# Offering the small instruction streams a place behind every dense product instead of behind every third

## The chip, the cores and the metric

The kernel runs on one core of one Trainium2 chip. The metric is the device time of one execution in microseconds (us), lower is better. The kernel before takes 2010.35 us (median of three runs, 2009.24 to 2010.55).

## What is computed

One layer of an encoder trunk in float32: 1024 tokens of width 1024, with 16 learned tokens in front.

```python
h = rmsnorm(h_res, norm1_w[l])
proj = h @ w_in[l]
(q, k, v, z, b_raw, a_raw, sc_b, sc_c, sc_x, gate_a, gate_b) = jnp.split(proj, SPLIT_POINTS, axis=-1)
o_dn = gated_deltanet_bidir(q, k, v, z, b_raw, a_raw, dn_conv_w[l], A_log[l], dt_bias[l], dn_norm_w[l])
y_a = o_dn @ w_branch_dn[l]
y_b = (sc_b * depthwise_conv_centred(sc_c * sc_x, sc_conv_w[l])) @ w_branch_sc[l]
merged = jax.nn.sigmoid(gate_a) * y_a + jax.nn.sigmoid(gate_b) * y_b
h_res = h_res + merged @ w_out[l]
h2 = rmsnorm(h_res, norm2_w[l])
gu = h2 @ w_gate_up[l]
h_res = h_res + (jax.nn.silu(gu[..., :D_FF]) * gu[..., D_FF:]) @ w_down[l]
```

The gated DeltaNet branch has 8 heads of 128 columns. For each head, q, k and v go through a five-tap convolution and SiLU; the sequence is cut into chunks; in each chunk a triangular system is solved, and a state matrix is carried from chunk to chunk, once forward and once backward:

```python
def step(S, inp):
    qk_c, qd_c, kd_c, u_c, w_c, gl_c = inp
    v_new = u_c - jnp.einsum("bhcd,bhde->bhce", w_c, S)
    o_c = (jnp.einsum("bhcd,bhde->bhce", qd_c, S)
           + jnp.einsum("bhij,bhje->bhie", qk_c, v_new))
    S = S * gl_c[..., None, None] + jnp.einsum("bhcd,bhce->bhde", kd_c, v_new)
    return S, o_c
```

## The kernel before

The change lies in the first stage, from the start to about 1061 us, which holds the input projection and the whole DeltaNet branch. The later stages (the branch projections, the output projection, the MLP) are not touched.

**Dense products.** The input projection is cut into units of 128 output columns. Each unit is computed in two or three runs over the tokens, 320 to 512 tokens wide (336, 320 and 384 for q, k and v; 322, 320 and 384 for two of the three short-convolution columns; 512 for the rest). One run is 24 matmuls into one PSUM bank: 8 pieces of the contraction, and for each the three products of high and low parts that stand for one float32 product. These matmuls are line L339, in `dense_steps`, which is a generator: it yields after every third matmul. ScalarE or VectorE then empties the bank.

**Streams.** Per head there are four generators that issue small work: `g_decay`, `g_norm` (transposes and Gram products of q and k), `g_inv` (the triangular inverse) and `g_scan` (the chunk recurrence, 8 steps per head, both directions in each step). Each yields the planned time at which its next piece may be issued. Of these the scan matters most here. In each step it issues, in this order: TensorE L805 and L808 (state times k and q), VectorE L815 (r), TensorE L820 (inverse times r), ScalarE L827 (w, two instructions) and L832 (v, two instructions), TensorE L837 (k times w, the state's increment) and L840 (the second part of the output), VectorE L849 (the new state) and then output work. L805, L820 and L837 write different columns of the same PSUM bank, `b1`; w and v are both read from the columns that L820 wrote. One float32 matmul of 128 columns runs as two passes, so a pair of them stands as four instructions in the trace.

**The order.** The order on every engine is the order in which the instructions are issued by the Python code; an engine executes its own in that order, and semaphores hold it where an operand is not ready. The code keeps four planned clocks `T`. `pe(ns)` advances that of TensorE and returns the time plus HOP = 200 ns; `V` and `A` advance VectorE's and ScalarE's by a cost for the width and return the end plus TOPE = 370 ns. A scan's wait between L820 and L837 reads so:

```python
            for d in range(2):
                mm(b1[:, 2 + d], NP[:, cd[d], d], r0[d], start=True, stop=True)
            yield pe(430)
```

and then w (whose last `A` gives the time that is yielded), v (whose time is not yielded), and the next yield. At every yield of a dense unit the main loop calls `run_streams`, which issues every stream's piece whose time has come by TensorE's planned clock, and `pump`, which fills VectorE with convolution and inverse work until it is planned 700 ns ahead. So a piece of a stream can stand only where a dense unit yields. The main loop also cuts the next unit's weights into high and low parts at four fixed yields of a unit, numbered in `SPL`: ScalarE L945 (wh), then VectorE L942 (wl), twice.

Of the kernel before, what the change touches and what calls it, by code (L numbers as in the profile page):

```python
# [47 lines left out]
def encoder_layer(ctx: ExitStack, tc: tile.TileContext, x, meta, norm1_w, w_in, w_ba,  # L48
# [22 lines left out]
    def psm():  # L71
        return ps.tile([P, 512], F32, tag="m", name=uid("pm"), bufs=2)
# [37 lines left out]
    def wtiles(shape):  # L110
        return [wp.tile(shape, F32R, tag=g, name=uid(g), bufs=2) for g in ("wh", "wl")]
# [158 lines left out]
    def pe(ns):  # L270
        T["pe"] += ns
        return T["pe"] + HOP

    def V(n, kind=0):
        return on("dve", (68 + 1.042 * n, 130 + 1.042 * n, 130 + 0.52 * n)[kind])

    def A(n):
        return on("act", 144 + 0.834 * n)
# [37 lines left out]
    def pump():  # L316
        while T["dve"] <= T["pe"] + 700:
            now = max(T["dve"], T["pe"])
            cand = [k for k, q in lanes.items() if q and q[0].ready <= now + 20]
            if not cand and any(q and q[0].ready <= now + DEP + 20 for q in lanes.values()):  # L320
                T["dve"] = now + DEP
                continue
            if not cand:
                return
            k = min(cand, key=lambda q: spent[q])
            spent[k] += lanes[k][0].step() * WEIGHT[k]
            if lanes[k][0].done:
                lanes[k].pop(0)

    sweep = ()  # L330

    def dense_steps(po, w, xx, t0, n):
        (wh, wl), (xh, xl) = w, xx
        t0 += C0
        parts = {"hh": (wh, lambda k: xh[:, k]), "hl": (wh, lambda k: xl[k]), "lh": (wl, lambda k: xh[:, k])}
        seq = [(m, k) for m in sweep for k in range(KT)] if sweep else [(m, k) for k in range(KT) for m in ("hh", "hl", "lh")]
        for i, (m, k) in enumerate(seq):
            ww, f = parts[m]
            mm(po[:, :n], ww[:, k], f(k)[:, t0:t0 + n], start=i == 0, stop=i == 3 * KT - 1)  # L339
            if i % 3 == 2:  # L340
                pe(3 * (n / 2.4 + 13))
                yield

    raws = []
# [6 lines left out]
    def half_buffer():  # L351
        return d1.tile([P, 520], F32, tag="rb", name=uid("rb"), bufs=3)
# [20 lines left out]
    def u_qkv(h, i, w):  # L373
# [9 lines left out]
        for ci, (t0, n) in enumerate(QCH):  # L383
            po = psm()
            yield from dense_steps(po, w, hx, t0, n)
            if raw is None:
                raw = row_buffer()
                nc.gpsimd.memset(raw[:, 0:2], 0.0)
                nc.gpsimd.memset(raw[:, L + 2:L + 4], 0.0)
            nc.scalar.copy(raw[:, 2 + t0:2 + t0 + n], po[:, :n])  # L390
            nc.scalar.activation(dst[:, t0:t0 + n], po[:, :n], AF.Copy, scale=wc[:, 2, col:col + 1])  # L391
            A(n)
            A(n)
            yield
            sub["rows"] = 2 + t0 + n if ci < 2 else L + 4
            if ci == 1:
                job = enqueue("conv", conv_job(raw, dst, col, sub, "t"))
                raws.append(job)
# [21 lines left out]
    def u_short(j, i, w):  # L420
        st_ = shorts[j]
        if i < 2:
            for t0, n in ((14, 322), (336, 320), (656, 384)):
                po = psm()
                yield from dense_steps(po, w, hx, t0, n)
                if "cx" not in st_:
                    st_["cx"] = row_buffer()
                    nc.gpsimd.memset(st_["cx"][:, 1026:1028], 0.0)
                    raws.append(Job(iter(())))
                sl = st_["cx"][:, t0 - 14:t0 - 14 + n]  # L430
                if i == 0:
                    nc.scalar.copy(sl, po[:, :n])
                    A(n)
                else:
                    nc.vector.tensor_tensor(out=sl, in0=po[:, :n], in1=sl, op=ALU.mult)
                    V(n)
            if i == 1:
                st_["yc"] = []
                st_["job"] = enqueue("conv", short_job(st_["cx"], j, st_["yc"]))
                raws[st_["ri"]] = st_["job"]  # L440
            else:
                st_["ri"] = len(raws) - 1
        else:
            for i2 in range(2):
                po = psm()
                yield from dense_steps(po, w, hx, META + 512 * i2, 512)
                force(st_["job"])
                yc = st_["yc"][i2][:, :512]
                nc.vector.tensor_tensor(out=yc, in0=po, in1=yc, op=ALU.mult)
                V(512)  # L450
                nc.sync.dma_start(p_d[j][:, 512 * i2:512 * i2 + 512], yc)
# [10 lines left out]
    def u_z(h, w):  # L462

        rest = None
        for i in range(2):
            po = psm()
            for k, _ in enumerate(dense_steps(po, w, hx, META + 512 * i, 512)):
                if k == 3 and rest:
                    rest()
                yield  # L470
            th = half_buffer()[:, :512]
            nc.scalar.activation(th, po, AF.Tanh, scale=0.5)
            A(512)

            def rest(i=i, th=th, po=po):
                nc.vector.scalar_tensor_tensor(out=th, in0=th, scalar=1.0, in1=po, op0=ALU.add, op1=ALU.mult)
                V(512)
                nc.sync.dma_start(z_d[h][:, 512 * i:512 * i + 512], th)
        T["dve"] = max(T["dve"], T["act"] + HOP)
        rest()  # L480
# [275 lines left out]
    def g_scan(h, st_):  # L756
# [141 lines left out]
        for c4 in range(2):  # L898
            oT = NP[:, 4 * c4:4 * c4 + 4, 1 - c4]
            pt = newbank()  # L900
            for c in range(4):
# [10 lines left out]
                 for h in range(H) for i, off in enumerate((OK, OQ, OV))]  # L912
    fill_units = [(off + j * P, lambda w, j=j, i=i: u_short(j, i, w), None, i)
                  for j in range(8) for i, off in enumerate((OSC, OSX, OSB))]
    fill_units += [(off + j * P, lambda w, j=j, d_=d_[j]: u_gate(j, d_, w), None, None)
                   for j in range(8) for off, d_ in ((OGA, ta_d), (OGB, tb_d))]
    fill_units += [(OZ + h * P, lambda w, h=h: u_z(h, w), None, None) for h in range(ZH)]
    done = freed = 0
    decs, norms, invs, scans = [], [], [], []
# [5 lines left out]
    def pick():  # L925

        mid = fill_units and fill_units[0][3] in (1, 2)
        if qkv_units and not mid and qkv_ok():
            u = qkv_units.pop(0)
        elif fill_units:  # L930
            u = fill_units.pop(0)
        else:
            return None
        raw = rawtile([P, KT, P])
        nc.sync.dma_start(raw, w_in[unit(u[0])])
        return [u, None, raw, [0]]

    def split_part(u, i):
        u[3][0] = i + 1
        k = slice(4 * (i // 2), 4 * (i // 2) + 4)  # L940
        if i % 2:
            nc.vector.tensor_tensor(out=u[1][1][:, k], in0=u[2][:, k], in1=u[1][0][:, k].bitcast(F32), op=ALU.subtract)  # L942
            V(512)
        else:
            nc.scalar.copy(u[1][0][:, k], u[2][:, k])  # L945
            A(512)
# [20 lines left out]
    def run_streams():  # L967
        nonlocal done
        again = True
        while again:  # L970
            again = False
            for q in (scans, invs, norms, decs):
                if q and q[0][1] <= T["pe"]:
                    again = True
                    r = next(q[0][0], None)
                    if r is None:
                        h = q.pop(0)[2]
                        if q is scans:
                            done += 1
                        elif q is not decs:  # L980
                            heads[h]["inverted" if q is invs else "normed"] = True
                    else:
                        q[0][1] = r
            start_streams()
# [335 lines left out]
                yield T["act"]  # L1320

    dn = ph1.enter_context(tc.tile_pool(name="dn", bufs=1))
    SPL = (11, 12, 13, 14)
    for g in (gen0, gen1):
        for _ in g:
            pass
    decs.append([g_gates(), T["pe"], None])
    while done < H or qkv_units or fill_units or any(ahead):
        u = ahead.pop(0)
        if u is None:  # L1330
            run_streams()
            pump()
            T["pe"] += 100
            ahead.append(pick())
            continue
        for k in range(u[3][0], 4):
            split_part(u, k)
        if ahead[0]:
            ahead[0][1] = wtiles([P, KT, P])
        ahead.append(pick())  # L1340
        for n_, _ in enumerate(u[0][1](u[1])):
            if ahead[0] and n_ in SPL:
                split_part(ahead[0], SPL.index(n_))
            run_streams()
            pump()
# [240 lines left out]
    for j in range(NF):  # L1586
# [9 lines left out]
        if j >= HK:  # L1596
            k = j - HK
# [176 lines left out]
```

## Time and profile before

| | |
|---|---|
| median of three runs | 2010.35 us |
| the profiled execution's own time | 2009.61 us |
| its span, first to last instruction | 2007.9 us |
| TensorE clock granted, mean | 0.999 |
| TensorE matmul busy | 1987.4 us, 99% of the span |
| VectorE busy | 1353.8 us, 67% |
| ScalarE busy | 823.9 us, 41% |
| dense products of the first stage (L339) | 4272 matmuls |

All times are from one profiled execution; a start time counts from its first instruction. In rows of the timeline the first two numbers are the start and the duration in us, then the engine (PE is TensorE's matmuls, PEld its weight loads, DVE VectorE, ACT ScalarE), the line, the instruction, what it writes and reads, the shape, the count of instructions merged into the row, and in brackets the engine's idle time before it and what ended that. A matmul's duration is longer than its distance to the next, because matmuls are pipelined; what counts is the distance between starts.

### The profile page before, as it was taken

Reading aid. Unit: us, or ns where it says so; the run is one execution under the profiler, and the core shown is the slowest. Engines: PE = TensorE matmul, PEld = TensorE weight load, DVE = VectorE, ACT = ScalarE, POOL = GpSimd, SP = SyncE. Lnnn points to the kernel's source line nnn. Section 1 sums busy time; section 2 is a strip of 40 time slices with the busy share of each in tenths; the row PEclk is TensorE's granted clock in tenths of the full one; section 3 lists DMA queues with packets and bytes.
Section 4 is the critical chain, followed back from the end, with each engine's and each line's share of the span. In section 5 each row is a group of like instructions: output and inputs, shape, how many; then the busy total and the mean of one; then the engine's idle time right before and its main releaser. Section 6 shows DMA issues by size and latency. Waiting matters only on the chain.

```text
span 2007.9 us, 31943 instructions
## 1 busy us (share of the span) xinstructions
PE 1987.4 (99%) x12059; PEld 1727.9 (86%) x12059; DVE 1353.8 (67%) x2966; ACT 823.9 (41%) x1945; POOL 119.6 (6%) x407
## 2 busy tenths in 40 slices
PE   9999999999999999999999999999999999999998
PEld 8999999999999988988888888887888888888887
DVE  6889586888888776866245434468866666646575
ACT  6462345454554464633334211224423333334344
POOL 2002200101020202010000000000000000000000
PEclk9999999999999999999999999999999999999999
DMA  3121222212212232232127633123666345477654
GB/s 138 40 88 64 75 78 71 74 47 76 59 54 85 69 101 64 81 89 94 70 94 247 215 126 116 58 90 109 237 225 221 139 149 186 158 272 244 196 172 167
DMA packets 131409, 247.85 MB, mean 123 GB/s; under 512 B 45045, under 2 KB 54694, under 8 KB 128823
## 3 DMA queue, kind: packets, MB, share of 16 engines
q1 hardware_dynamic: 130679, 244.77, 36.1%
q8 instruction: 94, 1.54, 0.3%
q10 hardware_dynamic: 576, 1.05, 0.1%
q14 instruction: 60, 0.49, 0.1%
HBM read 179.10 MB, written 66.67 MB: 122 GB/s over the span
## 4 chain that ended last, share of the span: by engine, by line
PE 90%; DVE 5%; ACT 2%; DMA 1%; issue 1%; SPq 0%; ACTq 0%; DVEq 0%
PE pm L339 36%; PE pd L1514 10%; PE pe L1514 4%; PE pm L1514 3%; PE pe L589 1%; PE pd L820 1%; PE pe L134 1%; PE pe L135 1%; PE pe L133 1%; PE pd L840 1%; PE pd L134 1%; PE pd L133 1%; PE pd L135 1%; PE pe L1682 1%; PE pe L1680 1%; PE pd L837 1%
## 5 line engine op out<-in xcount | busy, mean ns | idle before, releaser
L339 PE MATMUL pm<-hTh,wh 128*128 128x512 f32 (+4 forms) x1424 | 518.2, 369 | 0.8 <-ACT kq L391 0.5
L339 PE MATMUL pm<-hTh,wl 128*128 128x512 f32 (+4 forms) x1424 | 483.4, 344 | 0.0
L339 PE MATMUL pm<-al,wh 128*128 128x512 f32 (+4 forms) x1424 | 482.6, 343 | 0.0
L339 PEld LDWEIGHTS pm<-hTh,wh 128*128 128x128 f32 x1424 | 267.0, 188 | 20.4 <-issue 1.7
L339 PEld LDWEIGHTS pm<-hTh,wl 128*128 128x128 f32 x1424 | 266.1, 188 | 19.8 <-DVE wl L942 0.3
L339 PEld LDWEIGHTS pm<-al,wh 128*128 128x128 f32 x1424 | 267.4, 189 | 14.5
L101 DVE TENSOR_TENSOR al<-raw,ring_h 128x1024 fp32r<-128x1024 f32 x73 | 88.8, 1224 | 65.4 <-ACT ring_h L100 64.6
L942 DVE TENSOR_TENSOR wl<-raw,wh 128x512 fp32r<-128x512 f32 x134 | 91.0, 690 | 51.0 <-ACT wh L945 50.5
L100 ACT CAST ring_h<-raw 128x1024 fp32r<-128x1024 f32 x73 | 76.8, 1055 | 106.8 <-PE pd L1682 35.5
L361 DVE SCALAR_TENSOR_TENSOR kq<-ra,wc,kq 128x520 f32<-128x520 f32 x128 | 96.9, 757 | 3.3 <-ACT kq L391 1.7
L945 ACT CAST wh<-raw 128x512 fp32r<-128x512 f32 x134 | 79.2, 622 | 13.3 <-PE pm L339 9.6
L100 ACT CAST wh<-raw 128x1024 fp32r<-128x1024 f32 x43 | 45.2, 1052 | 85.8 <-PE pe L134 35.2
L827 ACT ACTIVATE w<-pd,small 128x128 f32<-128x128 f32 x128 | 40.2, 366 | 84.8 <-PE pd L820 79.7
L498 DVE TENSOR_TENSOR fP<-fP,tm 128x135 f32<-128x135 f32 (+23 forms) x248 | 71.3, 288 | 4.9
L494 DVE TENSOR_TENSOR tm<-fP,fN 128x135 f32<-128x135 f32 (+23 forms) x248 | 71.2, 287 | 4.4
L849 DVE SCALAR_TENSOR_TENSOR S<-S,eGl,pd 128x128 f32<-128x128 f32 x104 | 31.9, 345 | 52.0 <-PE pd L837 33.9
L1516 DVE TENSOR_TENSOR b<-pd,b 128x512 f32<-128x512 f32 x22 | 15.2, 691 | 68.5 <-PE pd L1514 68.5
L1617 ACT ACTIVATE b<-b 128x512 f32<-128x512 f32 x22 | 13.9, 633 | 114.8 <-DVE b L1516 114.8
L101 DVE TENSOR_TENSOR wl<-raw,wh 128x1024 fp32r<-128x1024 f32 x43 | 52.4, 1220 | 12.3 <-ACT wh L100 12.2
L664 POOL TENSOR_TENSOR tm<-mP,mN 1x15 f32<-1x15 f32 (+7 forms) x120 | 42.9, 358 | 218.7 <-DMA mN<-ndm 210.2
L1514 PE MATMUL pd<-b_hl,wh 128*128 128x512 f32 x176 | 54.4, 390 | 0.0
L361 DVE SCALAR_TENSOR_TENSOR vT<-ra,wc,vT 128x520 f32<-128x520 f32 x64 | 48.4, 756 | 3.6 <-ACT vT L391 2.6
(523 smaller groups left out, 4416.9 us busy)
## 6 DMA issues: line engine op xcount, KB each, us to landing
raw<-in_w_in_dram SPq DMA_DIRECT2D x72, 512.0 KB
raw<-in_w_gate_up_dram SPq DMA_DIRECT2D x44, 512.0 KB
sums<-in_w_down_dram SPq DMA_DIRECT2D x22, 512.0 KB
t_d<-sums SPq DMA_DIRECT2D x11, 1024.0 KB
raw<-s_d SPq DMA_DIRECT2D x44, 256.0 KB
raw<-t_d SPq DMA_DIRECT2D x44, 256.0 KB
act_d<-b SPq DMA_DIRECT2D x43, 256.0 KB
raw<-act_d SPq DMA_DIRECT2D x33, 256.0 KB
```

Source lines behind the costliest of these rows:

```text
L100: nc.scalar.copy(hi, src)
L101: nc.vector.tensor_tensor(out=lo, in0=src, in1=hi.bitcast(F32), op=ALU.subtract)
L133: mm(po[:m, :n], wh[:, k, :m], xhk[:, t0:t0 + n], start=(k == 0), stop=False)
L339: mm(po[:, :n], ww[:, k], f(k)[:, t0:t0 + n], start=i == 0, stop=i == 3 * KT - 1)
L361: nc.vector.scalar_tensor_tensor(out=acc, in0=raw[:, h0 + t:h0 + t + hn], scalar=wc[:, t, col:col + 1], in1=acc, op0=ALU.mult, op1=ALU.add)
L494: nc.vector.tensor_tensor(out=tv, in0=fP[:, 0:r, j:j + 1].broadcast_to([P, r, n]), in1=fN[:, j:j + 1, j + 1:32].broadcast_to([P, r, n]), o ...
L498: nc.vector.tensor_tensor(out=fP[:, 0:r, j + 1:32], in0=fP[:, 0:r, j + 1:32], in1=tv, op=ALU.subtract)
L664: nc.gpsimd.tensor_tensor(out=tv, in0=mP[:, 0:j + 1, j:j + 1].broadcast_to([1, j + 1, n]), in1=mN[:, j:j + 1, j + 1:META].broadcast_to([1, ...
L827: nc.scalar.activation(w[d], b1[:, 2 + d], AF.Copy, scale=ce[:, c, d:d + 1])
L942: nc.vector.tensor_tensor(out=u[1][1][:, k], in0=u[2][:, k], in1=u[1][0][:, k].bitcast(F32), op=ALU.subtract)
L945: nc.scalar.copy(u[1][0][:, k], u[2][:, k])
L1514: mm(po, x[:, k], y, start=k + i == 0 and not add_to, stop=k == 3 and i == 2, skip_group_check=add_to)
```

## The change

After the first head's preparations the dense generator yields after each matmul. Its planned time is added per matmul, with the same total. The numbers that name yields are trebled: the four at which weights are split (27 yields of a q, k or v unit become 75) and the one at which a z unit finishes its earlier half. Nothing is computed otherwise, and no instruction is added or taken away.

```diff
+    fine = {"on": False}
...
-            if i % 3 == 2:
-                pe(3 * (n / 2.4 + 13))
+            pe(n / 2.4 + 13)
+            if fine["on"] or i % 3 == 2:
                 yield
...
-                if k == 3 and rest:
+                if k == 11 and rest:
                     rest()
...
-    SPL = (11, 12, 13, 14)
+    SPL = (33, 36, 39, 42)
...
     decs.append([g_gates(), T["pe"], None])
+    fine["on"] = True
     while done < H or qkv_units or fill_units or any(ahead):
```

## The prediction

> **What bounds the kernel now.** I read the page first, then the busy time by stretches, TensorE's waits in the first stage, and the timeline of the scan's steps.
>
> ```profile
> PE 1987.4 (99%) x12059; PEld 1727.9 (86%) x12059; DVE 1353.8 (67%) x2966; ACT 823.9 (41%) x1945; POOL 119.6 (6%) x407
> ```
>
> ```profile
> 165.00:1061.00 896.00, 892.04 (x6916) 804.57 (x6915) 645.55 (x1874) 403.50 (x1251) 95.93 (x330) 1.00 0.24 75
> ```
>
> ```profile
> PE pd L820 <- DVE r L815: 3.4, 6, 0.8
> PE pd L837 <- ACT v L832: 0.2, 1, 0.2
> PE pm L339 <- ACT kq L391: 0.2, 1, 0.2
> ```
>
> The second row is the first stage after its start-up: in 896 us TensorE's matmuls are busy 892.04, VectorE 645.55 and ScalarE 403.50, at a granted clock of 1.00. The third block lists all that TensorE waited for there: 3.4 + 0.2 + 0.2 = 3.8 us (the columns are us, times, longest). So the stage lasts as long as TensorE's work plus its waits. Finer placement changes no matmul, so it can gain at most about these waits; it loses every wait it adds.
>
> Does the end of the streams set the end of the stage? The timeline's last stream work on TensorE and the stage's end:
>
> ```profile
> 1041.43 0.60 PE L97 MATMUL pd<-ident,NP 128*128 128x128 f32 x4
> ...
> 1060.72 0.39 PE L339 MATMUL pm<-hTh,wl 128*128 128x512 f32 x1
> 1060.95 0.39 PE L133 MATMUL pm<-hTh,wh 128*128 128x512 f32 x1
> ```
>
> The last head is done at 1042, and 19 us of pure dense work follow before the next stage's first matmul at 1060.95. Heads that finish earlier therefore bring nothing: dense work that filled between them moves behind them. Heads that finish up to 19 us later would cost nothing either.
>
> **Does a place between dense matmuls have a price of its own?** Here is a scan step in a 512 wide unit, from TensorE's timeline, then ScalarE's:
>
> ```profile
> 913.67 0.61 PE L805 MATMUL pd<-S,kq 128*128 128x128 f32 x4
> 914.11 0.61 PE L808 MATMUL pd<-S,kq 128*128 128x128 f32 x4
> ...
> 915.95 0.61 PE L820 MATMUL pd<-r,NP 128*128 128x128 f32 x4
> 916.32 0.48 PE L339 MATMUL pm<-hTh,wh 128*128 128x512 f32 x1
> 916.63 0.39 PE L339 MATMUL pm<-al,wh 128*128 128x512 f32 x1
> ...
> 918.25 0.40 PE L339 MATMUL pm<-hTh,wl 128*128 128x512 f32 x1
> 918.48 0.39 PE L837 MATMUL pd<-w,kn 128*128 128x128 f32 x2
> ```
>
> ```profile
> 916.65 0.63 ACT L827 ACTIVATE w<-pd,small 128x128 f32<-128x128 f32 x2 [2.05 <-DVE tm L494]
> 917.16 0.63 ACT L832 ACTIVATE v<-pd,small 128x128 f32<-128x128 f32 x2
> ```
>
> Four passes in a row take 914.11 - 913.67 = 0.44 us. Alone between dense matmuls (915.95 to 916.32, and the next dense matmul coming 0.31 instead of 0.23 later, 0.23 being 918.48 - 918.25) they take 0.37 + 0.31 - 0.23 = 0.45. Splitting insertions over more places is thus free to 0.01 us each; even 300 more places, about as many as there are insertions now, would be 3 us, and I take 0 to 3 with 0.5 as likeliest, since most pieces stand alone already.
>
> **The step that gets a wait: L820 to L837.** In these rows nine dense matmuls lie between L820 and L837. The planned clocks give just that: one dense matmul counts 512/2.4 + 13 = 226 ns, a yield comes each 679. Counted from L820's planned end, w may be issued from 200 on, so at 679; two w cost 2 x 251; 370 are added: 1551, and the next yield is 2037, nine matmuls. With a yield each 226: w at 226, L837 from 1098 on, so at 1131, five matmuls. The same sums give 9 before and 8 after at 384, 336 and 320 (there the old yields lay closer: 3 x 146 = 439 at 320, w at 439, L837 from 1311 on, at 1317).
>
> Is there room for it? Not for v. The plan yields w's time, but the trace shows that L837 is held by v:
>
> ```profile
> L837 PE MATMUL pd<-w,kn x224: 270/275/377, 238.1 to 1024.0; 128*128 128x128 f32 x112
> its engine sat idle before it (us, times) until:
>   ACT v L832: 2.4, 11
> ```
>
> That is the view of line L837 alone: its 224 passes are 56 groups of four, and all its waits were ended by v (the view counts the weight loads too, hence more than the 0.2 above). The order of v and L837 is the same in the changed kernel, so the same semaphore holds it there. The Trainium skill, page "PSUM — Partial Sum Buffer", section "PSUM bank collisions raise a hardware error", says why: TensorE may not write a bank while ScalarE reads it, even at other columns, so semaphores go by the bank. The trace agrees with its 11 waits for v, which L837 does not read; by this rule every L837 has to wait so in the changed kernel as well.
>
> How late is v? At 320 wide:
>
> ```profile
> 802.68 0.60 PE L820 MATMUL pd<-r,NP 128*128 128x128 f32 x4
> 803.04 0.39 PE L339 MATMUL pm<-hTh,wh 128*128 128x320 f32 x1
> ...
> 804.15 0.31 PE L339 MATMUL pm<-al,wh 128*128 128x320 f32 x1
> 804.30 0.31 PE L339 MATMUL pm<-hTh,wl 128*128 128x320 f32 x1
> 804.57 0.71 PE L837 MATMUL pd<-w,kn 128*128 128x128 f32 x4
> ```
>
> ```profile
> 803.89 0.63 ACT L832 ACTIVATE v<-pd,small 128x128 f32<-128x128 f32 x2
> ```
>
> v ends at 803.89 + 0.63 = 804.52, and L837 starts 0.05 later: it waited. Its own place was 804.30 + 0.15 = 804.45. After a wait its four passes take 0.71 instead of the 0.61 of L820 above, so a wait costs 0.10 more than its length.
>
> Now the sum. At 512, v ends at 917.16 + 0.63 = 917.79, L837 can start at 917.84. Four matmuls earlier than 918.48 is 918.48 - 4 x 0.23 = 917.56: a wait of 0.28, with the 0.10 a loss of 0.38 us where there was none. At 320 the wait exists already and grows by one dense matmul, 0.15. For 336 and 384:
>
> ```profile
> 816.88 0.32 PE L339 MATMUL pm<-hTh,wl 128*128 128x336 f32 x1
> 817.04 0.71 PE L837 MATMUL pd<-w,kn 128*128 128x128 f32 x4
> ```
>
> ```profile
> 816.36 0.63 ACT L832 ACTIVATE v<-pd,small 128x128 f32<-128x128 f32 x2
> ```
>
> ```profile
> 569.10 0.34 PE L339 MATMUL pm<-hTh,wl 128*128 128x384 f32 x1
> 569.27 0.49 PE L837 MATMUL pd<-w,kn 128*128 128x128 f32 x3
> ```
>
> ```profile
> 568.45 0.63 ACT L832 ACTIVATE v<-pd,small 128x128 f32<-128x128 f32 x2
> ```
>
> At 336, v allows 817.04, just where L837 stands: one matmul earlier loses 0.15 to 0.16. At 384, v allows 569.13 and one matmul earlier is 569.10: 0.03, with part of the 0.10, say 0.06. There are 8 heads with 7 such pairs, the 56 groups above; read off the timeline one by one (L837 at 238.1 is the first, at 1024.0 the last), 22 start in 512 wide runs, 16 in 320 or 322, 9 in 336 and 9 in 384. Loss: 22 x 0.38 + 16 x 0.15 + 9 x 0.15 + 9 x 0.06 = 8.4 + 2.4 + 1.4 + 0.5 = 12.7 us. Bounds: where ScalarE is planned late by an eviction, the place may not move, so as little as half, 6; if all runs behave as 512, 56 x 0.38 = 21.
>
> **The hops over VectorE.** L805 to L820 goes over r, L837 to the next L805 over the new state.
>
> ```profile
> 914.36 0.60 DVE L815 SCALAR_TENSOR_TENSOR r<-pd,negEG,vS 128x128 f32<-128x128 f32 x2
> ```
>
> ```profile
> 711.03 0.60 DVE L815 SCALAR_TENSOR_TENSOR r<-pd,negEG,vS 128x128 f32<-128x128 f32 x2
> ...
> 711.69 0.71 PE L820 MATMUL pd<-r,NP 128*128 128x128 f32 x4 [0.84 <-DVE r L815]
> ```
>
> r ends at 914.96 and L820 starts at 915.95: a margin of 0.99. The plan (r's end 527 past L808's planned end, plus 370, so 897) puts L820 behind the fourth matmul instead of the sixth: 0.53 remains, so VectorE must be half a microsecond late to matter. The second block is such a case, r behind a weight split. The 3.4 us above are six of these, 0.57 each. With the margin smaller by 0 to 0.46 (it stays at six matmuls for 336 and 384), those six grow by about 0.25 and some four more appear at 0.3 with 0.10 each: 1.5 + 1.6, so 3 us; 0 if the waits at L837 give VectorE time to catch up, 8 if all 64 hops lose on average 0.12. The inverse and the norm have some 8 x 5 more hops with margins that I did not see under 0.1: 0 to 4, taken as 0.5. The weight splits stay at the same matmul for q, k and v and move up two matmuls elsewhere, with the same distances: nothing; no DMA issue moves by more than a matmul or two for it.
>
> **Sum.** 12.7 + 3 + 0.5 + 0.5 = 16.7 us. The profiled execution took 2009.61; 2026.3. The median lies 0.74 above that, so 2027.0.
>
> **Rivals.** The changes that a measurement of this kernel can tell from none begin at about 0.2%, 4 us.
>
> Faster: pieces issued closer to their planned time give ScalarE and VectorE their work earlier, so that operands are ready earlier too, and the 3.8 us of waits go with the 0.10 behind each of the six: 2006. It decides if w and v end earlier by as much as L837 moves up. For it: w is issued up to 0.45 earlier in the plan. Against: ScalarE already starts w when L820 lets it (the 2.05 idle in front of w above), so v cannot end earlier. A page speaks for still more: the Trainium skill, "Perfetto Trace Analysis", section "Identifying the Most-Contended Engine", judges TensorE by weight-load busy time, which is 804.57 of 896, so some 90 us would be open.
>
> ```profile
> 917.33 0.19 PEld L339 LDWEIGHTS pm<-hTh,wl 128*128 128x128 f32 x1
> ```
>
> But a weight load of 0.19 for a matmul each 0.23 is 83% in a stretch without any gap, so this measure shows width and no gap here. Chance 0.10.
>
> No change: pieces are held by ScalarE's planned clock and not by the yields, so the pairs stay where they are; only the hops over VectorE lose: 2010.35 + 3 = 2013. For it: in 15 of the 56 pairs more than nine matmuls lie between, behind an eviction or a tanh. Against: 41 stand at exactly nine, as the yields give. Chance 0.10.
>
> Much slower: the chain runs faster (at 512 six and nine matmuls of a step become four and five), convolution and inverse work are drawn together, VectorE, 645.55 of 896 busy, falls behind its plan, and its hops stall. It decides once r or the state is late by over 0.5 at most steps. If a quarter of the 120 hops stalls by today's 0.57 + 0.10, that is 20 us more: 2047. Against it: after a stall VectorE has caught up. Chance 0.10.
>
> **How the numbers follow.** The forecast case has 0.70: its own range from the bounds is 6 + 0 to 21 + 8 + 4 + 3, 2016 to 2046, mostly 2018 to 2036. The range of 8 in 10 reaches to the no-change case and part of the last: 2013 to 2040. Slower by over 0.2%: forecast, much slower and part of no change, 0.84; within 0.06; faster 0.10.
>
> **What would show it.** Right: in the changed kernel L837 waits for v in nearly all 56 pairs, with five dense matmuls of 512 or eight of the narrower ones between; its row of waits rises from 0.2 to near 10 us; the last head ends before 1042 while the stage ends some 16 us after 1061; later stages last as before. Wrong: nine matmuls between them still, waits without v, or a stage that ends by 1061.

## The result, and the profile after

The changed kernel takes 2032.26 us (median of four runs, 2030.55 to 2035.14) against 2010.45 us before: a ratio of 1.0111, 95% interval 1.0095 to 1.0127. It is 21.8 us slower; forecast were 2027.0 us in a range of 2013 to 2040. The profiled execution is the longest of the four: it took 2035.14 us, with a span of 2033.4.

The lines of the first stage are renumbered by one: the dense matmuls are L340, L805 is L806, r is L816, L820 is L821, w L828, v L833, the state product L837 is L838, L840 is L841, the new state L850. First the end of the stage, from TensorE's timeline: the last stream's work, and the first matmul of the next stage (L133).

```profile
974.01 0.60 PE L97 MATMUL pd<-ident,NP 128*128 128x128 f32 x4
...
1082.82 0.39 PE L340 MATMUL pm<-hTh,wl 128*128 128x512 f32 x1
1083.05 0.39 PE L133 MATMUL pm<-hTh,wh 128*128 128x512 f32 x1
```

The heads are done 67 us earlier (974 instead of 1041), and yet the stage ends at 1083.05 instead of 1060.95: 22.1 us later. The two profiled spans are 25.5 us apart (2033.4 and 2007.9); the other 3.4 lie in what follows, which takes 950 us here and 947 before, though its code is the same (946 to 951 in most of the variants below). The 21.8 us between the medians are about what the stage lost. So the chain of heads became faster and the stage slower, as a stage does that TensorE's work plus its waits fill.

The stretch of the stage, and the waits as the profile lists them:

```profile
165.00:1083.00 918.00, 907.82 (x6926) 804.15 (x6925) 639.10 (x1869) 400.44 (x1249) 91.38 (x322) 1.00 0.24 73
```

```profile
PE pd L821 <- DVE r L816: 2.8, 9, 0.5
PE pe L590 <- DVE PQ L617: 1.5, 1, 1.5
PE pd L806 <- DVE S L850: 1.4, 3, 0.5
PE pm L340 <- DVE wl L943: 0.8, 1, 0.8
PE pd L793 <- DVE w L791: 0.3, 1, 0.3
PE pm L340 <- issue: 0.3, 1, 0.3
```

The second list sums to 7.1 us and v does not stand in it at all. A matmul's row lasts longer than its distance to the next, so a wait that begins under such a tail is no idle time of TensorE's matmuls. The view of one line counts the idle time in front of the weight loads too, and there the waits show. A wait that outlasts the tail stands in it twice, once at the weight load and once at the matmul: the 29 times of r below are 20 places, 9.0 us by the weight loads alone. The 40 of v are 40 places, since they stand at weight loads only. These are the views of L838, L821 and L806 in the changed kernel (us, times):

```profile
its engine sat idle before it (us, times) until:
  ACT v L833: 16.0, 40
```

```profile
its engine sat idle before it (us, times) until:
  DVE r L816: 11.7, 29
```

```profile
its engine sat idle before it (us, times) until:
  DVE S L850: 3.9, 7
```

Before, v had 2.4 us in 11 waits, r 9.7 in 16 (10 places, 6.2 us by the weight loads) and the state none. And this is a scan step in a 512 wide unit, TensorE and then ScalarE:

```profile
947.49 0.60 PE L821 MATMUL pd<-r,NP 128*128 128x128 f32 x4
947.85 0.47 PE L340 MATMUL pm<-al,wh 128*128 128x512 f32 x1
...
948.86 0.39 PE L340 MATMUL pm<-hTh,wl 128*128 128x512 f32 x1
949.38 0.38 PE L838 MATMUL pd<-w,kn 128*128 128x128 f32 x1
```

```profile
948.70 0.63 ACT L833 ACTIVATE v<-pd,small 128x128 f32<-128x128 f32 x2
```

Five dense matmuls stand between L821 and L838. The fifth starts at 948.86, so L838's place was 949.09; v ends at 948.70 + 0.63 = 949.33, and L838 starts 0.05 later. It waited 0.29 us.

For the sizes below I went through the starts of all TensorE's matmuls up to the end of the stage, and took for each pair of neighbours how far their distance lies above the undisturbed one of such a pair (a wait's after-effect on its next pass counts with it):

| us lost | before | changed |
|---|---|---|
| state product, behind v | 2.7 | 13.6 |
| product with the inverse, behind r | 5.8 | 8.0 |
| L806, behind the state | 0 | 2.9 |
| the norm's Gram products | 0.4 | 2.9 |
| transposes | 2.7 | 5.2 |
| first matmul of a dense run and the rest | 3.9 | 8.1 |

The first five rows grow by 21.0 us, and the stage grew by 22.1, so the last row's 4.2 is about 3 too much. Where shortened distances are set against lengthened ones, the five stay much as they are (10.7, 2.1, 2.8, 2.9 and 2.5 us) and the rest grows by about 1.

### The profile page after: what moved, and what is told of

Read it like the earlier page. It is cut to its first block, busy times and chain, and to the rows that moved or that the text cites. A ratio compares the mean times of both kernels' runs of the same rounds, so it can differ in the third digit from the quotient of the medians.

```text
span 2033.4 us, 31971 instructions
## 1 busy us (share of the span) xinstructions
PE 2003.9 (99%) x12059; PEld 1727.0 (85%) x12059; DVE 1348.3 (66%) x2966; ACT 819.7 (40%) x1945; POOL 116.2 (6%) x407
## 4 chain that ended last, share of the span: by engine, by line
PE 49%; DVE 2%; DMA 2%; ACT 1%; issue 0%; SPq 0%; ACTq 0%; DVEq 0%
PE pd L1516 10%; PE pm L340 6%; PE pe L1516 4%; PE pm L1516 3%; PE pe L135 1%; PE pe L134 1%; PE pe L133 1%; PE pd L135 1%; PE pd L134 1%; PE pd L133 1%; PE pe L1684 1%; PE pe L1682 1%; PE pe L1683 1%; PE pd L1684 1%; PE pd L1682 1%; PE pd L1683 1%
## 5 line engine op out<-in xcount | busy, mean ns | idle before, releaser
L340 PE MATMUL pm<-al,wh 128*128 128x512 f32 (+4 forms) x1424 | 496.5, 353 | 0.0
L340 PE MATMUL pm<-hTh,wh 128*128 128x512 f32 (+4 forms) x1424 | 493.4, 351 | 1.1 <-ACT ra L433 0.4
L340 PE MATMUL pm<-hTh,wl 128*128 128x512 f32 (+4 forms) x1424 | 493.3, 351 | 0.8 <-DVE wl L943 0.8
L340 PEld LDWEIGHTS pm<-hTh,wh 128*128 128x128 f32 x1424 | 266.7, 188 | 19.4 <-issue 1.1
L340 PEld LDWEIGHTS pm<-hTh,wl 128*128 128x128 f32 x1424 | 267.1, 188 | 18.8 <-DVE wl L943 1.5
L340 PEld LDWEIGHTS pm<-al,wh 128*128 128x128 f32 x1424 | 267.0, 188 | 17.4 <-issue 0.2
L362 DVE SCALAR_TENSOR_TENSOR kq<-ra,wc,kq 128x520 f32<-128x520 f32 x128 | 97.0, 758 | 9.0 <-ACT kq L392 6.7
L828 ACT ACTIVATE w<-pd,small 128x128 f32<-128x128 f32 x128 | 40.0, 363 | 101.3 <-PE pd L821 97.6
L850 DVE SCALAR_TENSOR_TENSOR S<-S,eGl,pd 128x128 f32<-128x128 f32 x104 | 31.9, 344 | 54.8 <-PE pd L838 19.9
L101 DVE TENSOR_TENSOR wl<-raw,wh 128x1024 fp32r<-128x1024 f32 x43 | 52.4, 1219 | 12.7 <-ACT wh L100 12.6
L533 ACT ACTIVATE PQ<-PQ,negG 128x128 f32<-128x128 f32 x128 | 43.3, 394 | 16.4 <-DVE PQ L528 16.2
```

The costliest lines, as they stand in the source:

```text
L101: nc.vector.tensor_tensor(out=lo, in0=src, in1=hi.bitcast(F32), op=ALU.subtract)
L362: nc.vector.scalar_tensor_tensor(out=acc, in0=raw[:, h0 + t:h0 + t + hn], scalar=wc[:, t, col:col + 1], in1=acc, op0=ALU.mult, op1=ALU.add)
L533: nc.scalar.activation(PQ[:, c, d], PQ[:, c, d], AF.Exp, bias=negG2[:, c, hd:hd + 1])
```

## The experiments

**Which half of the change loses it.** The change lets both the streams' pieces and VectorE's filling happen behind every matmul. Two runs take one back each. Streams at thirds:

```diff
+            fine["third"] = i % 3 == 2
             if fine["on"] or i % 3 == 2:
                 yield
...
-            run_streams()
+            if fine["third"]:
+                run_streams()
             pump()
```

> The changed kernel, but the streams are offered a place behind every third matmul only, while VectorE's filling (pump) runs behind every one. Theory (lost margin of the streams' places): 2009 to 2015 us, state products nine matmuls behind L820 again. Rival A (price of a place): 2009 to 2012 us as well. Rival B (VectorE filled too far ahead): the loss stays, 2025 us or more.

Measured: 2016.37 us, ratio to before 1.0033 (1.0021 to 1.0046). Filling at thirds (the same edit around `pump()` instead):

> The changed kernel, but pump runs behind every third matmul only, while the streams are offered a place behind every one. Theory (lost margin): v's waits stay at about 16 us; those for r and the state shrink a little, 2026 to 2032 us. Rival A: 2030 to 2034 us. Rival B (VectorE filled too far ahead): the loss goes, 2010 to 2016 us.

Measured: 2032.88 us, 1.0110 (1.0095 to 1.0126). Taking the streams' places back returns some 16 of the 22 us; the finer filling that is left then costs some 6, more than the theory had it (2009 to 2015). Taking the filling back alone returns nothing, and this run too lies above the theory's range (by 0.9 us, within that of rival A). So the two halves do not add up: with the streams at every matmul the filling makes no difference, with the streams at thirds it makes 6 us. What those 6 us are was not tried. The waits for v follow the streams: the view of the state product (L839 in both) has with the streams at thirds

```profile
its engine sat idle before it (us, times) until:
  ACT v L834: 3.4, 15
```

and with the filling at thirds

```profile
its engine sat idle before it (us, times) until:
  ACT v L834: 16.9, 45
```

The rival that each place between dense matmuls has a price falls here, because the places hardly become more: the stage has 357 insertions between dense matmuls before, 360 in the changed kernel and 371 with the filling at thirds. What one place costs was not measured by any of these runs.

**Giving the margin back.** The planned hops get 0.45 us more, all of them or VectorE's alone:

```diff
-    HOP, TOPE, DEP = 200, 370, 127
+    HOP, TOPE, DEP = 200, 820, 127
```

> The changed kernel with TOPE raised from 370 to 820 ns, so that every planned hop over ScalarE and VectorE has 0.45 us more. Theory (lost margin): the waits at the products behind v, r and the state all go, some 16 of the 22 us come back, 2008 to 2016 us; the heads end later than in the changed kernel (974 us), but before the dense work does. Rival A (price of a place): 2030 us or more. Rival B (VectorE filled too far ahead): r and the state still come late, 2025 us or more, since more margin in the plan does not shorten VectorE's queue.

Measured: 2014.25 us, 1.0020 (1.0010 to 1.0029): 18 of the 22 us come back with the same fine places. The pairs of L821 and L838 are as far apart as before again: 591 dense matmuls lie in the 56 of them, against 438 in the changed kernel and 576 before. The views of L838 and L821 there:

```profile
its engine sat idle before it (us, times) until:
  ACT v L833: 0.6, 3
```

```profile
its engine sat idle before it (us, times) until:
  DVE r L816: 8.0, 18
```

The waits for v are all but gone; those for r are down from 11.7 to 8.0, below the 9.7 of before, and did not go as the theory had said. For VectorE alone:

```diff
-        return T[e] + TOPE
+        return T[e] + (820 if e == "dve" else TOPE)
```

> The changed kernel with 0.45 us more margin for the planned ends of VectorE alone (820 instead of 370 ns); ScalarE's stay. The first four runs left open why the waits behind v (13.6 us with what follows them) gave back only some 3 us when they were removed. Theory C (the waits move: TensorE, released from v, meets VectorE's lateness at the next hop, so one margin alone gives back less than its waits): the waits for v stay at 12 to 16 us, those for r and the state shrink to a third, 2022 to 2027 us; with the 3 us of v's time alone that is less than the 18 us of both margins together. Theory D (VectorE's lateness is all there is, and v's wait only fills time in which VectorE catches up): 2013 to 2018 us.

Measured: 2025.23 us, 1.0074 (1.0059 to 1.0089). Theory D falls, and the waits for v remain and even grow:

```profile
its engine sat idle before it (us, times) until:
  ACT v L833: 22.2, 52
```

This run and the one with all hops differ by the margin of ScalarE and GpSimd alone, by 11.0 us in time and by 22.2 against 0.6 us in the waits for v.

**v's wait, taken away in two ways.** First by the plan:

```diff
                 nc.scalar.activation(v2[d], b1[:, 2 + d], AF.Copy, scale=cc[:, c, d:d + 1])
-                A(P)
+                t = A(P)
```

> The changed kernel, but the scan's wait behind v gives v's planned end instead of w's, so the state product (the former L837) is placed some 0.5 us later in the plan. Theory (lost margin, above all at the product that v holds): its 16.0 us of waits in 40 places fall to under 3 us, the stage is shorter by about 11 us, the time is 2019 to 2024 us. Rival A (each place between dense matmuls has a price, and there are more places): the places stay as many, 2030 to 2034 us. Rival B (VectorE is filled further ahead, since it is filled at each matmul): 2030 to 2034 us.

Measured: 2029.36 us, 1.0095 (1.0080 to 1.0110), 3 us where 8 to 13 were expected, although no state product waits for v any more. L821 and L806 there:

```profile
its engine sat idle before it (us, times) until:
  DVE r L816: 17.9, 32
```

```profile
its engine sat idle before it (us, times) until:
  DVE S L850: 6.9, 12
```

The waits for r rose from 11.7 to 17.9 us (still in 20 places) and those for the state from 3.9 to 6.9. Then without touching the plan, by writing to another bank:

```diff
-                mm(b1[:, 2 + d], NP[:, cd[d], d], r0[d], start=True, stop=True)
+                mm(b2[:, 2 + d], NP[:, cd[d], d], r0[d], start=True, stop=True)
...
-                mm(b2[:, 2 + d], PQ[:, cd[d], d], v2[d], start=True, stop=True)
+                mm(b1[:, 2 + d], PQ[:, cd[d], d], v2[d], start=True, stop=True)
```

with the readers of both changed to match.

> The changed kernel with the same plan, but the product with the inverse (the former L820) is written into the other bank of the step, and the last product of the step (the former L840) into the bank of the state product; so the state product writes a bank that v does not read. If it is the shared bank that holds it behind v: its waits for v (16.0 us, 40) go though the plan is the same, and by theory C the waits move to VectorE's hops, 2024 to 2031 us. If v held it in another way: the waits stay, 2030 to 2035 us. A cost of its own: the new state is read from the bank that the last product writes, so VectorE may wait for that, up to 0.45 us in 56 places.

Measured: 2021.00 us, 1.0053 (1.0038 to 1.0068), 11.3 us below the changed kernel and more than expected. The places are the same: 438 dense matmuls lie in the 56 pairs of both kernels. A step here, TensorE and ScalarE:

```profile
935.62 0.40 PE L340 MATMUL pm<-hTh,wl 128*128 128x512 f32 x1
935.86 0.61 PE L838 MATMUL pd<-w,kn 128*128 128x128 f32 x4
```

```profile
935.47 0.63 ACT L833 ACTIVATE v<-pd,small 128x128 f32<-128x128 f32 x2
```

v ends at 935.47 + 0.63 = 936.10 and the state product has started at 935.86, while v was still running, and its four passes last 0.61 us again. In this kernel 38 of the 56 state products start before v ends, in the changed kernel none. So v held it through the bank that they shared, and taking that away is worth 11.3 us net. (Before and after the change, the state product writes the same columns as the step's first product, not others as the section on the kernel has it; v reads those of the product with the inverse. In the program a bank is one tile, so the run does not tell a wait by bank from one by tile.) The edit has a cost of its own: the second product of a step, L809, now waits for output work of the step before,

```profile
its engine sat idle before it (us, times) until:
  DVE NP L871: 9.4, 35
```

and in that time r gets ready, so that the waits for r fall to 0.2 us in the view of L821. About 8 us changed places so; the waits for the state rose from 3.9 to 6.4.

The two ways differ by 8 us, and one run has both edits:

> The changed kernel with both the other bank (2021.0 us alone, same places as the changed kernel) and v's planned end given by the scan's wait (2029.4 us alone). No state product waits for v in either. Open is why v's time alone gave back 3 us and the other bank 11. Theory E (v's time moves all the later places against the other streams and the weight splits, and those places happen to be worse: r, the state, the norm's Gram products and the inverse wait some 10 us more): the bad places are there here too, 2026 to 2031 us. Theory C (a wait taken away at v comes back at VectorE's hops whatever the places): with the waits gone already, later places only add margin, 2017 to 2022 us.

Measured: 2030.73 us, 1.0100 (1.0083 to 1.0117). Theory E: the later places that v's time gives cost some 10 us elsewhere, whether or not v waits. By the same count as in the table, the Gram products lose 5.5 us there (1.4 with the other bank alone), the product with the inverse 2.6 (0.3); the small products that build the inverse lose some 4 more as well.

**Is it the weight splits?** Eight of the 20 late r seemed to stand right behind a VectorE half of a split (wl), which waits for ScalarE's half. By the trace it is seven, with 2.9 of the 11.7 us.

```diff
-    SPL = (33, 36, 39, 42)
+    SPL = (21, 33, 34, 46)
```

> The changed kernel with the weight splits' ScalarE and VectorE halves twelve matmuls apart instead of three (places 21, 33, 34 and 46 instead of 33, 36, 39 and 42), so that VectorE does not wait for ScalarE's half (71.0 us in 30 places now). If VectorE's lateness behind the splits is a main part of the loss (8 of the 20 waits for r stand right behind one): 2022 to 2028 us. If it only shows there by chance: 2030 to 2034 us.

Measured: 2031.91 us, 1.0107 (1.0091 to 1.0124): no gain. VectorE's waits in its own list went from the first row to the second,

```profile
DVE wl L943 <- ACT wh L946: 71.0, 30, 9.6
```

```profile
DVE wl L943 <- ACT wh L946: 59.2, 19, 5.0
```

but those at r hardly moved (11.7 to 10.5 us). As an experiment on VectorE's wait it is weak, since 59.2 of the 71.0 us stayed. But only three late r still stand behind a split, and nothing was gained, so the splits are not a main part of the loss. The larger group was overlooked: in both kernels nine late r stand right behind a convolution instruction of VectorE's filling (L362), with 7.1 of the 11.7 us in the changed kernel and 6.5 of the 10.5 here.

**More margin, and a faster version.** Both margins at once (TOPE 820 and v's time):

> The changed kernel with TOPE 820 and v's planned end given by the scan's wait: both margins at once. Lost margin: the rest of the waits for v (0.8 us) goes, those for r and the state stay as with TOPE 820 alone, 2009 to 2014 us. If moving the places by itself changes the waits elsewhere by several us, as v's time alone seemed to do: anywhere from 2008 to 2020 us.

Measured: 2019.28 us, 1.0041 (1.0026 to 1.0056), the second of the two outcomes. TOPE 1270:

> The changed kernel with TOPE 1270, so 0.9 us more margin at each hop than before the change. Lost margin: the waits for r and the state (7.3 us left at TOPE 820) shrink further, 2006 to 2012 us; the last head ends at about 1045 us, still before the dense work. If what is left is not a matter of margin: 2012 to 2016 us. If the heads end after the dense work, TensorE idles at the end of the stage: 2015 us or more.

Measured: 2016.45 us, 1.0030 (1.0019 to 1.0041). Both are slower than TOPE 820 alone, so more margin does not go on helping: with TOPE 820 and v's time, the transposes lose 8.7 us (6.0 with TOPE 820 alone). With TOPE 1270 the last head ended at 1070 us instead of the 1045 that I expected, after the next stage's first product at 1059; yet TensorE did not idle there (39.99 us busy from 1040 to 1080). The kernel before with TOPE 820:

> The kernel before (a place behind every third matmul) with TOPE 820. Its waits for r and v (some 8 us with what follows them) shrink, but its last head ends 19 us before the dense work only, and 0.45 us more at some 50 hops a head makes the chain longer than that: with an end of the heads after about 1062 us TensorE runs out of dense work, 2010 to 2030 us. If the longer chain still ends in time: 2004 to 2008 us.

Measured: 2011.79 us, 1.0004 (0.9994 to 1.0014), no difference that the runs can tell. The kernel before with v's time alone:

> The kernel before with v's planned end given by the scan's wait instead of w's. Its waits for v (2.7 us with what follows them) go; the pairs move one group of three matmuls apart at most. Lost margin: 2006 to 2010 us, the same or a little faster; the heads end later than 1042 us, and if they end after 1060 TensorE stands idle for the rest: then 2012 us or more.

Measured: 2007.75 us, 0.9988 (0.9979 to 0.9998): the one version below both kernels, by 0.1%. With an interval that ends just under 1, among twelve variants, this is a hint and not a gain that is shown. No state product waits for v in it, and TensorE's list of waits is down to

```profile
PE pd L820 <- DVE r L815: 1.7, 5, 0.5
PE pe L589 <- DVE PQ L616: 0.4, 1, 0.4
PE pd L741 <- DVE XT L733: 0.3, 1, 0.3
```

## Why the prediction was right, point by point

**TensorE's work and waits fill the stage, and earlier heads bring nothing.** Right: the heads ended 67 us earlier and the stage 22.1 us later. The waits before were read too small, though: the 3.8 us are those of TensorE's matmul rows alone. By its weight loads r was late in ten places for 6.2 us, and v in ten for 2.2.

**A place has no price of its own.** Not put to the test: there were three more insertions in all, instead of the 300 that I allowed for, so the term was nothing whatever a place costs.

**The state product behind v, 12.7 us.** Right in mechanism and size. Five dense matmuls lie between in 17 of the 19 pairs at 512, eight in 26 of the 37 narrower ones, and 47 of 56 start within 0.08 us of v's end. The loss by the table is 13.6 - 2.7 = 10.9 us, and the other bank took off 11.3. The term was somewhat too large because only 17 pairs, and not 22, came to five matmuls at 512, so the pairs there lost 6.2 us instead of 8.4. The narrower ones lost 4.7 us more than before, against 4.3 in the sum, although in 11 of them 11 to 13 matmuls lie between, the case that bounded the term from below.

**The hops over VectorE, 3 us.** Too small: 2.2 for r and 2.9 for the state, 5.1. I had seen no wait for the state and gave it no share. And r was late in ten places before, not in six; after the change it was late in 20, and the state in four.

**The inverse and the norm, 0.5 us.** This is the term that was missed most: Gram products 2.5 and transposes 2.5 more, and about 1 in all the rest. I had set their margins at over 0.1 us without a row, and said so. The forecast was 5 us short in all: the hops over VectorE, the inverse and the norm were some 7 us too small together, and that the state product's term was 2 too large hid a part of it, which is luck.

**The rivals.** Much slower through VectorE needed a quarter of the 120 hops late by 0.67 us; 24 were late, ten before, and r and the state lost 5.1 us more. No change needed pairs held by ScalarE's plan: 11 of 56. Faster needed v earlier; it ends 1.8 us after L821's start, as before (949.33 - 947.49).

**What was to be seen.** One sign was wrong: the list of TensorE's waits would show v near 10 us. It shows none; the view of the line does. And v was to hold nearly all 56 pairs: it holds 40, and 47 start within 0.08 us of its end.

**What stays open.** That margin gives back 18 us is shown, and that v's wait is some 11 of them (the other bank, and the margin of ScalarE and GpSimd). Why one set of places costs 8 to 10 us more than another in which no product waits for v is not: the runs show only that it goes with the places (v's time with and without the other bank) and not with the bank or the splits. Why the finer filling costs 6 us with the streams at thirds and nothing with them at every matmul is open too.

## What to carry to other kernels

In an order planned ahead, the grid of places is itself a margin: rounding up to the next third matmul had hidden that one planned time was that of w, where the next product must also wait for v in the same bank. Before making a grid finer, check for each placed instruction what really releases it, bank neighbours too, and then try more than one remedy: v's own time in the plan returned 3 us here, another bank 11, more margin on all hops 18. In a stage that one engine fills, a faster chain beside it is worth nothing, as the heads that ended 67 us earlier show. A change of margins also moves all later places, so judge it by several variants and not by the wait that it removes.

## What the runs showed of the hardware that was not expected

- A wait of a product for a semaphore costs more than its length: in the changed kernel the four passes of L838 last 0.71 us (median) in the 47 groups that start within 0.08 us of v's end, 0.61 in the nine others, and the next dense matmul comes 0.10 us later too.
- The end of the stage was less of a wall than I took it for, though this is the kernel's doing and not the chip's. In the kernel before with TOPE 820 the last head ends at 1079, 30 us after the next stage's first product at 1049, and yet TensorE was busy for 39.62 of the 40 us from 1040 to 1080; the next stage's first products had moved in between the scan's.

```profile
1040.00:1080.00 40.00, 39.62 (x226) 33.19 (x225) 18.71 (x65) 15.02 (x48) 0.00 (x0) 1.00 0.14 46
```
